# First FFN: smaller budgets for the side work per block and token tile, a booked adaLN extraction, and a defer shorter by one

## The chip, the cores and the metric

The kernel runs on one core of a Trainium2 chip. The metric is the device time of one execution in microseconds (us); three timed runs of the kernel before are shown below, and one execution was recorded by the hardware profiler. In the views PE is TensorE's matmul, DVE is VectorE, ACT is ScalarE, POOL is GpSimd and SP is SyncE, which issues most loads. DMAs are also issued from ScalarE's queue (ACTq in the rows).

## The reference, cut to what matters

One layer of a diffusion backbone over 1024 latent tokens and 256 context tokens, width 1024, in float32. The change lies in the first half-step SwiGLU (hidden width 2816) and in work that is done beside it:

```python
mx = adaln(c, w_mod[l], b_mod[l])            # nine rows of 1024: shift, scale, gate, three times
mc = adaln(c_ctx[None], w_mod[l], b_mod[l])
x = x + 0.5 * mx[2] * swiglu(modulate(x, g_ffn1[l], mx[0], mx[1]), w_gu1[l], w_down1[l])
ctx = ctx + 0.5 * mc[2] * swiglu(modulate(ctx, g_ffn1[l], mc[0], mc[1]), w_gu1[l], w_down1[l])
hx = modulate(x, g_mix[l], mx[3], mx[4])
...
x = x + mx[5] * mix_x                        # mixer: latent attention beside a bidirectional S5
x = x + 0.5 * mx[8] * swiglu(modulate(x, g_ffn2[l], mx[6], mx[7]), w_gu2[l], w_down2[l])
```

where `swiglu(h)` is `(silu(gate) * up) @ w_down` with `gate, up = split(h @ w_gu)`. The S5 branch needs tables of powers of its 16 x 64 complex states for both directions, made from parameters alone.

## The kernel before, in words

**The first FFN.** 1280 tokens are ten tiles of 128; three blocks `XB` hold four, four and two tiles. The hidden width is cut into `NF` = 22 blocks of 128, numbered f. For each f, gate and up (`gu`) are made transposed, 128 hidden rows by up to 512 tokens, over eight slices of the width. Each float32 product is three matmuls of high and low parts (`mm3`, L621 to L623 of the profile; wH, wL are a weight's parts, aH, aL those of an activation, hH, hL, shown as big, those of the input). ScalarE takes silu out of the gate's bank (sg), VectorE multiplies the up's bank into it (`sg<-gu,sg`), and ScalarE and GpSimd split the result. For every second f a `down` multiplies two hidden blocks by their down weights: ten tiles, two halves of 512 columns each, six matmuls for each half, and after each half VectorE adds the bank to the accumulator (`acc<-dn,acc`). In the loop, gate of f comes first, then the down of f-2 and f-1, if f is even, then the up of f. The last down, of f = 20 and 21 together (joint), comes behind the loop.

**The side work.** A generator `gen` in `ffn1_mix_in` holds the work that isn't the FFN's. First comes `adaln_rest`: seven rows of modulation (chunks 2 to 8), for which weight rows wmr are loaded and added, scaled, into ad on VectorE; TensorE sums over partitions (adp), and for the shift and scale rows `extract` multiplies by the identity and reduces (adm, then col). Then comes `s5_pre`: the power tables, and eight chunks of two S5 groups. A chunk makes a header (bc, B), a table T (six VectorE operations), for each direction d six products on GpSimd (tam, o1m, o2m) in turn with six on VectorE (taa, o1a, o2a), and a copy rep. `finish` of a direction then transposes and multiplies on TensorE (s5p, s5k), copies to me and R on ScalarE, and `store`, `diagonal` and `store_k` follow as deferred calls: three DMAs to d_s for a direction and four more for T, three small VectorE operations, and fifteen DMAs of R.

**What hands it out.** `pump(credit, cap)` adds to a credit, up to the cap, and runs the generator until the credit is spent; each `yield` names a price. It is called after each gu block with tiles * GURATE, and after each tile of a down with DNRATE. `defer(n, fn)` puts a call off by n calls of `side()`, one of which follows most pumps and each tile of a down. Before a chunk's header and before each direction's products the generator is held (`held`) until the finish before it has run. `drain()` runs all that is left at once. `at(20, 0)`, between the down of f = 20 and its up, drains, opens the pools of the gates g and of the residual rows xr in the memory that the side work's pools leave, and makes `prescale` the new generator: for each of ten tiles acc is multiplied by the gate and xr is added. `at(21, 1)` drains that, and the joint down follows.

Every instruction keeps its place in its engine's queue; nothing is reordered at run time.

Of the kernel before, what the change touches and what calls it, by code (L numbers as in the profile page):

```python
# [39 lines left out]
XLAG = 2  # L40
TLAG = 6
XB = [(0, 4), (4, 4), (8, 2)]
GURATE, DNRATE = 1.3, 1.2
SCRATCH = 512
PADR = 288

# [1 line left out]
class Kernel:  # L48
# [133 lines left out]
    def adaln_rest(self, pool):  # L182
        nc = self.nc
        wr, cols = {}, {}
        gates = (2, 5, 8)
        jobs = [(c, kt) for c in range(2, 9) for kt in range(KT + (c in gates))]

        def fetch(i):
            if i < len(jobs):
                c, kt = jobs[i]  # L190
                rows = (self.a["w_mod"][kt * 128:(kt + 1) * 128] if kt < KT else self.a["b_mod"])[:, c * D:(c + 1) * D]
                w = pool.tile([rows.shape[0], D], F32, tag="wmr", name="wmr", bufs=3)
                nc.sync.dma_start(w, rows)
                wr[i] = w

        def reduce(chunk, s, acc):
            row = chunk in gates
            m = pool.tile([1, D] if row else [128, D], F32, tag=f"adm{s}", name="adm")
            for h in range(2):
                p, hs = self.bank(self.free, "adp"), slice(h * 512, (h + 1) * 512)  # L200
                nc.tensor.matmul(p, lhsT=self.ones, rhs=acc[:, hs], start=True, stop=True)
                if row:
                    nc.scalar.activation(out=m[:, hs], in_=p[0:1, :], func=AF.Copy, scale=1.0 if chunk == 5 else 0.5)
                else:
                    nc.scalar.copy(m[:, hs], p)
            if row:
                self.defer(1, lambda: nc.scalar.dma_start(self.d_gate[chunk, s], m))
            else:
                self.defer(2, lambda: extract(chunk, s, m))

        def extract(chunk, s, m):
            c = self.cst.tile([128, KT], F32, name=f"col{chunk}{s}")
            v = m.rearrange("p (k f) -> p k f", k=KT)
            self.tt(v, v, self.ident[:, None, :].to_broadcast([128, KT, 128]), MUL)
            nc.vector.tensor_reduce(out=c, in_=v, axis=AX.X, op=ADD)
            self.tt(c, c, self.bcol[:, chunk, :], ADD)
            cols[chunk, s] = c
            if chunk in (4, 7):
                self.set_mod(1 if chunk == 4 else 2, s, cols[chunk - 1, s], c)

        fetch(0)
        fetch(1)
        accs = None
        for i, (chunk, kt) in enumerate(jobs):
            sets = (0, 1) if chunk <= 4 else (0,)
            if kt == 0:
                accs = [pool.tile([128, D], F32, tag=f"ad{s}", name=f"ad{s}") for s in sets]
            for s in sets:
                yield 1.2
                if s == 0:  # L230
                    fetch(i + 2)
                if kt == 0:
                    self.ts(accs[s], wr[i], self.sc[:, kt, s:s + 1], MUL)
                elif kt < KT:
                    self.stt(accs[s], wr[i], self.sc[:, kt, s:s + 1], accs[s], MUL, ADD)
                else:
                    self.tt(accs[s][0:1, :], accs[s][0:1, :], wr[i], ADD)
            wr.pop(i)
            if i + 1 == len(jobs) or jobs[i + 1][0] != chunk:
                for s in sets:  # L240
                    fn = lambda chunk=chunk, s=s, acc=accs[s]: reduce(chunk, s, acc)
                    self.defer(2 + s, fn)
                self.held = fn
                yield 2.5 * len(sets)
        while self.late:
            self.held = self.late[-1][1]
            yield 0.0


    def s5_pre(self, st):  # L250
# [185 lines left out]
        for c in range(G // GC):  # L436
# [35 lines left out]
            for d in range(2):  # L472
# [38 lines left out]
                def finish(d=d, dst=dst, M1=M1, M2=M2, AB=AB, AB2=AB2, rep=rep, T=T, Rs=Rs, c=c):  # L511
                    p = self.bank(self.free, "s5p")
                    for g in range(GC):
                        for i, X in enumerate((AB, AB2)):
                            nc.tensor.transpose(p[:, g * 256 + i * 128:g * 256 + i * 128 + 128],
                                                X[:, g].rearrange("p t c -> p (t c)"), self.ident)
                    me = pool.tile([128, GC, 256], F32, tag="me", name="me")
                    nc.scalar.copy(me.rearrange("p g n -> p (g n)"), p)
                    pk = self.bank(self.free, "s5k")
                    for g in range(GC):  # L520
                        nc.tensor.matmul(pk[:, g * 128:(g + 1) * 128], lhsT=rep[:, g].rearrange("p t c -> p (t c)"),
                                         rhs=M1[:, g, d:d + 8].rearrange("p t c -> p (t c)"), start=True, stop=True)
                    R = pool.tile([128, GC, 128], F32, tag=f"R{d}", name=f"R{d}")
                    nc.scalar.copy(R.rearrange("p g n -> p (g n)"), pk[:, 0:GC * 128])
                    Rs.append(R)
                    o = 1 - d

                    def store():
                        if d == 0:
                            for g in range(GC):  # L530
                                for h in range(2):
                                    nc.scalar.dma_start(
                                        dst[64 * h:64 * h + 64, g, O_T:O_T + 4 * NSEQ],
                                        T[64 * g:64 * g + 64].rearrange("p d r i j -> p (d r i j)"))
                        for i, X in enumerate((M1, M2)):
                            nc.scalar.dma_start(dst[:, :, O_C + d * 256 + i * 128:O_C + d * 256 + (i + 1) * 128],
                                                X[:, :, o:o + 8].rearrange("p g t c -> p g (t c)"))
                        nc.scalar.dma_start(dst[:, :, O_E + d * 256:O_E + d * 256 + 256], me)

                    def diagonal():  # L540
                        R0, R1 = Rs
                        self.tt(R0[:, :, 0:CH], R0[:, :, 0:CH], R1[:, :, 112:128], ADD)
                        for g in range(GC):
                            q = c * GC + g
                            self.stt(R0[:, g, 0:CH], mask, dsk[:, q:q + 1], R0[:, g, 0:CH], MUL, ADD)

                    def store_k():
                        R0, R1 = Rs
                        for s in range(8):
                            rows = slice(16 * s, 16 * s + 16)  # L550
                            nc.scalar.dma_start(dst[rows, :, O_K + 16 * s:O_K + 128], R0[rows, :, 0:128 - 16 * s])
                            if s:
                                nc.scalar.dma_start(dst[rows, :, O_K:O_K + 16 * s], R1[rows, :, 16 * (7 - s):112])

                    self.defer(1, store)
                    if d:
                        self.defer(2, diagonal)
                        self.defer(3, store_k)

                self.defer(4, finish)  # L560
                last = finish
        while self.late:
            self.held = self.late[-1][1]
# [89 lines left out]
    def ffn(self, blocks, hT, w_gu, w_dn, acc, P, hook=None, side=None, at=None, preload=None, keep=False, joint=False, start=None, pairs=0):  # L653
# [88 lines left out]
        for f in range(NF):  # L742
# [16 lines left out]
            else:  # L759
                sg = {}  # L760
                for b in nblk:
                    sg[b] = silu(b, gu(f, 0, b))
                    self.pump(blocks[b][1] * GURATE, 6.0)
                    if side:
                        side()
                load(f + 1, 0)
# [11 lines left out]
                    side()  # L778
                for b in nblk:
                    act[b] = act_of(f, b, sg[b], gu(f, 1, b))  # L780
                    self.pump(blocks[b][1] * GURATE, 6.0)
                    if side and f < NF - 2:
                        side()
                load(f + 1, 1)
# [10 lines left out]
    def ffn1_mix_in(self, srow):  # L795
# [24 lines left out]
        with ExitStack() as sact:  # L820
            actp = self.pool(sact, "act")
            with ExitStack() as sw:
# [75 lines left out]
                def at(f, phase):  # L898
                    if f == NF - 2 and phase == 0:
# [11 lines left out]
                        def prescale():  # L911
                            load(0)
                            load(1)
                            yield 4.0
                            for i, t in enumerate(order):
                                load(i + 2)
                                self.tt(acc[t], acc[t], g[int(t >= NX)], MUL)
                                yield 1.4
                                self.tt(acc[t], acc[t], xr.pop(i), ADD)
                                yield 1.4  # L920

                        self.gen = prescale()
                    elif f == NF - 1 and phase == 1:
# [901 lines left out]
```

## Time and profile before

| | us |
|---|---|
| three runs, median (lowest to highest) | 2546.02 (2544.89 to 2550.65) |
| profiled execution | 2544.01 |
| its span | 2542.2 |
| TensorE busy in the span | 2427.4 (95%) |
| VectorE busy | 1434.2 (56%) |
| granted TensorE clock, mean | 0.99 |

The profiled execution's time is that of the whole run; its span is the time from the first to the last recorded instruction, to which the times in the rows refer. TensorE's matmuls overlap: a row's duration runs from one matmul's start to its own modelled end, and the next starts before that.

### The profile page before, as it was taken

To read this page: it belongs to the slowest core of one execution; us is meant where nothing else is said; L and a number is where in the kernel's file an instruction comes from. 1 tells how busy PE (TensorE), PEld (TensorE's weight loads), DVE (VectorE), ACT (ScalarE), POOL (GpSimd) and SP (SyncE) were. 2 spreads that over 40 slices of the span, in tenths; PEclk is the share of its full clock that TensorE was granted. 3 is DMA by queue.
4 is the path that set the end of the run, shared out by engine and by line. 5 is a ranking of instruction groups with operands and counts; after the bars stand their busy time and mean duration, and the time that the engine had idled before them with its cause. 6 is when DMAs were issued, how large, how long until landed. Compare 5 with 4: busy or idle time off the path is not lost. (4 is left out here: it accounts for less than half of the span.)

```text
span 2542.2 us, 31980 instructions
## 1 busy us (share of the span) xinstructions
PE 2427.4 (95%) x12100; PEld 2004.9 (79%) x12100; DVE 1434.2 (56%) x2480; ACT 816.1 (32%) x1570; POOL 1036.1 (41%) x947
## 2 busy tenths in 40 slices
PE   7999998999999999898999999999999999999998
PEld 4788777888888887787777777777788888888886
DVE  3667578345434537747788888863344444444443
ACT  4311211211121112533677777762411111111112
POOL 2422314433433333426576666755433223323222
PEclk9999999999999999899999999999999999999999
DMA  7234621222222123316000000113211111111111
GB/s 283 86 106 135 205 83 38 71 70 59 75 71 71 57 79 126 123 38 192 23 17 4 14 14 25 38 66 126 75 44 49 50 50 50 50 45 46 50 42 67
DMA packets 83544, 185.14 MB, mean 73 GB/s; under 512 B 22199, under 2 KB 41911, under 8 KB 82366
## 3 DMA queue, kind: packets, MB, share of 16 engines
q1 hardware_dynamic: 59990, 163.93, 19.3%
q10 hardware_dynamic: 23400, 19.16, 2.6%
q8 instruction: 95, 1.56, 0.3%
q14 instruction: 59, 0.48, 0.1%
HBM read 155.52 MB, written 27.54 MB: 72 GB/s over the span
## 5 line engine op out<-in xcount | busy, mean ns | idle before, releaser
L62 POOL TENSOR_TENSOR wL<-raw,wH 128x1024 fp32r<-128x1024 f32 x130 | 313.8, 2418 | 787.6 <-ACT wH L616 776.5
L62 DVE TENSOR_TENSOR acc<-dn,acc 128x512 f32<-128x512 f32 x516 | 350.4, 690 | 352.3 <-PE dn L623 352.1
L621 PE MATMUL gu<-big,wH 128*128 128x512 f32 (+1 forms) x1056 | 379.9, 360 | 3.0 <-ACT sg L720 1.5
L623 PE MATMUL gu<-big,wL 128*128 128x512 f32 (+1 forms) x1056 | 374.8, 355 | 2.3 <-POOL wL L62 2.3
L622 PE MATMUL gu<-big,wH 128*128 128x512 f32 (+1 forms) x1056 | 374.6, 355 | 1.8 <-POOL big L62 1.8
L621 PE MATMUL dn<-wH,aH 128*128 128x512 f32 x792 | 314.6, 397 | 18.9 <-DVE acc L62 14.1
L623 PE MATMUL dn<-wH,aL 128*128 128x512 f32 x792 | 311.3, 393 | 1.0 <-POOL aL L62 1.0
L622 PE MATMUL dn<-wL,aH 128*128 128x512 f32 x792 | 311.4, 393 | 0.0
L616 ACT ACTIVATE wH<-raw 128x1024 fp32r<-128x1024 f32 x130 | 136.3, 1055 | 497.9 <-DVE raw L62 226.5
L62 DVE TENSOR_TENSOR sg<-gu,sg 128x512 f32<-128x512 f32 (+1 forms) x110 | 69.8, 635 | 391.7 <-PE gu L623 369.6
L622 PE MATMUL gu<-hL,wH 128*128 128x512 f32 x704 | 274.5, 390 | 4.3 <-POOL hL L62 3.0
L621 PE MATMUL gu<-hH,wH 128*128 128x512 f32 x704 | 274.6, 390 | 0.0
L623 PE MATMUL gu<-hH,wL 128*128 128x512 f32 x704 | 273.9, 389 | 0.0
L62 POOL TENSOR_TENSOR aL<-sg,aH 128x512 fp32r<-128x512 f32 (+1 forms) x110 | 140.4, 1277 | 277.5 <-ACT aH L616 275.0
L621 PEld LDWEIGHTS gu<-big,wH 128*128 128x128 f32 x1056 | 200.1, 189 | 36.0 <-issue 4.1
L623 PEld LDWEIGHTS gu<-big,wL 128*128 128x128 f32 x1056 | 199.9, 189 | 31.5 <-POOL wL L62 3.4
L622 PEld LDWEIGHTS gu<-big,wH 128*128 128x128 f32 x1056 | 200.1, 189 | 31.1 <-POOL big L62 2.2
L616 ACT ACTIVATE aH<-sg 128x512 fp32r<-128x512 f32 (+1 forms) x110 | 64.7, 589 | 461.6 <-DVE sg L62 425.0
L621 PEld LDWEIGHTS dn<-wH,aH 128*128 128x128 f32 x792 | 150.5, 190 | 54.4 <-DVE acc L62 15.8
L62 DVE TENSOR_TENSOR ptL<-pt,ptH 128x512 fp32r<-128x512 f32 x240 | 162.8, 686 | 52.2 <-ACT ptH L1417 51.7
L623 PEld LDWEIGHTS dn<-wH,aL 128*128 128x128 f32 x792 | 150.6, 190 | 33.6 <-POOL aL L62 1.4
L622 PEld LDWEIGHTS dn<-wL,aH 128*128 128x128 f32 x792 | 150.9, 191 | 31.1 <-issue 0.5
(317 smaller groups left out, 4635.7 us busy)
## 6 DMA issues: line engine op xcount, KB each, us to landing
raw<-in_w_gu SPq DMA_DIRECT2D x86, 512.0 KB, 3.4
wmr<-in_w_mod SPq DMA_DIRECT2D x56, 512.0 KB, 4.5
raw<-in_w_down SPq DMA_DIRECT2D x44, 512.0 KB, 3.3
row<-d_s SPq DMA_DIRECT2D x16, 576.0 KB, 4.0
wm<-in_w_mod SPq DMA_DIRECT2D x8, 1024.0 KB, 7.1
d_s<-T ACTq DMA_DIRECT2D x32, 160.0 KB, 2.7
ck<-d_s SPq DMA_DIRECT2D x16, 320.0 KB, 4.0
acc<-in_x SPq DMA_DIRECT2D x8, 512.0 KB
```

Of the source, the lines that this page charges most:

```text
L62: (eng or self.nc.vector).tensor_tensor(out=out, in0=a, in1=b, op=op)
L616: self.nc.scalar.activation(out=H, in_=raw, func=AF.Copy)
L621: mm(out, lhsT=AH, rhs=BH, start=start, stop=False)
L622: mm(out, lhsT=AH, rhs=BL, start=False, stop=False)
L623: mm(out, lhsT=AL, rhs=BH, start=False, stop=stop)
```

## The change

Two rates are lowered (per tile of a gu block 1.3 to 1.1, per tile of a down 1.2 to 0.9), and the cap of a gu block goes from 6.0 to 4.0. `extract` now books 2.7 from the credit and `diagonal` 0.6, where they booked nothing; a scaled add of adaLN is priced 1.5 instead of 1.2. `finish` is put off by three calls of `side()` instead of four. The prices in `prescale` fall from 4.0, 1.4 and 1.4 to 3.0, 1.0 and 1.0. No operation is added or removed; the side work's instructions stand elsewhere among those of the FFN. The second FFN has no generator. The whole diff:

```diff
--- before.py
+++ after.py
@@ -40,7 +40,7 @@
 XLAG = 2
 TLAG = 6
 XB = [(0, 4), (4, 4), (8, 2)]
-GURATE, DNRATE = 1.3, 1.2
+GURATE, DNRATE = 1.1, 0.9
 SCRATCH = 512
 PADR = 288
 
@@ -211,6 +211,7 @@
         def extract(chunk, s, m):
             c = self.cst.tile([128, KT], F32, name=f"col{chunk}{s}")
             v = m.rearrange("p (k f) -> p k f", k=KT)
+            self.credit -= 2.7
             self.tt(v, v, self.ident[:, None, :].to_broadcast([128, KT, 128]), MUL)
             nc.vector.tensor_reduce(out=c, in_=v, axis=AX.X, op=ADD)
             self.tt(c, c, self.bcol[:, chunk, :], ADD)
@@ -226,7 +227,7 @@
             if kt == 0:
                 accs = [pool.tile([128, D], F32, tag=f"ad{s}", name=f"ad{s}") for s in sets]
             for s in sets:
-                yield 1.2
+                yield 1.5
                 if s == 0:
                     fetch(i + 2)
                 if kt == 0:
@@ -539,6 +540,7 @@
 
                     def diagonal():
                         R0, R1 = Rs
+                        self.credit -= 0.6
                         self.tt(R0[:, :, 0:CH], R0[:, :, 0:CH], R1[:, :, 112:128], ADD)
                         for g in range(GC):
                             q = c * GC + g
@@ -557,7 +559,7 @@
                         self.defer(2, diagonal)
                         self.defer(3, store_k)
 
-                self.defer(4, finish)
+                self.defer(3, finish)
                 last = finish
         while self.late:
             self.held = self.late[-1][1]
@@ -760,7 +762,7 @@
                 sg = {}
                 for b in nblk:
                     sg[b] = silu(b, gu(f, 0, b))
-                    self.pump(blocks[b][1] * GURATE, 6.0)
+                    self.pump(blocks[b][1] * GURATE, 4.0)
                     if side:
                         side()
                 load(f + 1, 0)
@@ -778,7 +780,7 @@
                     side()
                 for b in nblk:
                     act[b] = act_of(f, b, sg[b], gu(f, 1, b))
-                    self.pump(blocks[b][1] * GURATE, 6.0)
+                    self.pump(blocks[b][1] * GURATE, 4.0)
                     if side and f < NF - 2:
                         side()
                 load(f + 1, 1)
@@ -911,13 +913,13 @@
                         def prescale():
                             load(0)
                             load(1)
-                            yield 4.0
+                            yield 3.0
                             for i, t in enumerate(order):
                                 load(i + 2)
                                 self.tt(acc[t], acc[t], g[int(t >= NX)], MUL)
-                                yield 1.4
+                                yield 1.0
                                 self.tt(acc[t], acc[t], xr.pop(i), ADD)
-                                yield 1.4
+                                yield 1.0
 
                         self.gen = prescale()
                     elif f == NF - 1 and phase == 1:
```

The first place is VectorE's queue in the down of f = 6, where the tiles' evictions `acc<-dn,acc` and the adaLN sums of a chunk alternate. Before:

```order
L62 TENSOR_TENSOR acc<-dn,acc 128x512 x2
L69 SCALAR_TENSOR_TENSOR ad_2390<-wmr,sc,ad_2390 128x1024
L62 TENSOR_TENSOR adm<-adm,ident 128x1024
L215 TENSOR_REDUCE col_2462<-adm 128x8
L62 TENSOR_TENSOR col_2462<-col_2462,bcol 128x8
L69 SCALAR_TENSOR_TENSOR ma_2466<-col_2462,gcol 128x8
L62 TENSOR_TENSOR acc<-dn,acc 128x512 x2
```

In the changed kernel, the same down:

```order
L62 TENSOR_TENSOR acc<-dn,acc 128x512 x4
L69 SCALAR_TENSOR_TENSOR ad_2370<-wmr,sc,ad_2370 128x1024
L62 TENSOR_TENSOR acc<-dn,acc 128x512 x2
L69 SCALAR_TENSOR_TENSOR ad_2370<-wmr,sc,ad_2370 128x1024
L62 TENSOR_TENSOR acc<-dn,acc 128x512 x4
L69 SCALAR_TENSOR_TENSOR ad_2370<-wmr,sc,ad_2370 128x1024
```

The product with the identity, the reduce and the two short column operations behind it have left this place; scaled adds stand alone between evictions.

The second place is the end of the down of f = 20 on TensorE, where its last matmuls meet the up (gu) of f = 20, and where `at(20, 0)` drains. Before:

```order
L621 MATMUL dn<-wH_7237,aH_7366 128x512
L622 MATMUL dn<-wL_7238,aH_7366 128x512
L623 MATMUL dn<-wH_7237,aL_7367 128x512
L621 MATMUL gu<-big,wH_7372 128x512
L622 MATMUL gu<-big,wH_7372 128x512
L623 MATMUL gu<-big,wL_7373 128x512
```

In the changed kernel, whose line numbers here are higher by two:

```order
L624 MATMUL dn<-wL_7052,aH_7186 128x512
L625 MATMUL dn<-wH_7051,aL_7187 128x512
L516 MATMUL s5p<-ident,o1a 128x128
L516 MATMUL s5p<-ident,o2a 128x128
L516 MATMUL s5p<-ident,o1a 128x128
L516 MATMUL s5p<-ident,o2a 128x128
L522 MATMUL s5k<-o1m,rep 128x128 x2
L516 MATMUL s5p<-ident,o1a 128x128
L516 MATMUL s5p<-ident,o2a 128x128
L516 MATMUL s5p<-ident,o1a 128x128
L516 MATMUL s5p<-ident,o2a 128x128
L522 MATMUL s5k<-o1m,rep 128x128 x2
```

Three finishes (four transposes and the kernel products each, of directions 1, 0 and 1) now stand between dn and gu.

The third place is ScalarE's queue there. Before, it has the last stores of R of chunk 7 (d_s_7), and then the splits of f = 20 and 21 and the silu of f = 21 (L720):

```order
L551 DMA d_s_7_114<-R_7251 32x1x16
L553 DMA d_s_7_114<-R_7467 32x1x112
L616 ACTIVATE wH_7670<-raw 128x1024
L616 ACTIVATE aH_7700<-sg 128x512
L616 ACTIVATE aH_7737<-sg 128x512
L616 ACTIVATE aH_7775<-sg 128x256
L616 ACTIVATE wH_7785<-raw 128x1024
L720 ACTIVATE sg<-gu 128x512 x2
L720 ACTIVATE sg<-gu 128x256
```

In the changed kernel the rows are these; they begin with the last two stores of R of chunk 6 (d_s_6), and the fifteen stores of R of chunk 7 follow them, ahead of wH and aH:

```order
L553 DMA d_s_6_113<-R_7337 32x1x16
L555 DMA d_s_6_113<-R_7523 32x1x112
L519 COPY me<-s5p 128x512
L525 COPY R_7594<-s5k 128x256
L533 DMA d_s_7_114<-T 64x640 x4
L537 DMA d_s_7_114<-o1m 256x1x128
L537 DMA d_s_7_114<-o2m 256x1x128
L539 DMA d_s_7_114<-me 256x1x256
L519 COPY me<-s5p 128x512
L525 COPY R_7633<-s5k 128x256
L537 DMA d_s_7_114<-o1m 256x1x128
L537 DMA d_s_7_114<-o2m 256x1x128
```

What stood at this place, the splits of f = 20, now stands behind both chunks' stores.

## Rows read from the trace of the kernel before

**Rows 1.** The page's first line.

```profile
span 2542.2 us, 31980 instructions
```

**Rows 2.** Windows: stretch, length, busy PE, PEld, DVE, ACT, POOL, clock, DMA share, GB/s.

```profile
105.00:450.00 345.00, 327.16 (x1533) 267.78 (x1532) 250.12 (x470) 55.80 (x85) 98.34 (x83) 0.98 0.35 114
450.00:956.60 506.60, 506.60 (x2569) 432.53 (x2569) 218.94 (x394) 85.36 (x140) 198.58 (x163) 1.00 0.24 72
956.60:1001.00 44.40, 42.80 (x222) 36.09 (x220) 33.25 (x27) 7.45 (x13) 15.81 (x9) 1.00 0.36 117
```

**Rows 3.** PE's waits, 100 to 450: total us, times, longest.

```profile
PE dn L621 <- DVE acc L62: 14.1, 4, 7.6
```

**Rows 4.** PE's timeline: start, us, engine, line, operation, count, [idle before <-releaser].

```profile
135.88 0.40 PE L621 MATMUL dn<-wH,aH 128*128 128x512 f32 x1
...
176.86 1.88 PE L201 MATMUL adp<-ad,ones 128*128 128x512 f32 x4
178.18 0.79 PE L621 MATMUL gu<-big,wH 128*128 128x512 f32 x1
...
424.06 0.79 PE L621 MATMUL dn<-wH,aH 128*128 128x512 f32 x1 [7.59 <-DVE acc L62]
...
472.68 0.27 PE L515 MATMUL s5p<-ident,o1a 128*128 128x128 f32 x1
...
473.48 0.36 PE L621 MATMUL gu<-big,wH 128*128 128x256 f32 x1
...
504.87 0.40 PE L621 MATMUL dn<-wH,aH 128*128 128x512 f32 x1
...
589.02 0.40 PE L621 MATMUL dn<-wH,aH 128*128 128x512 f32 x1
```

**Rows 5.** DVE's timeline: reduce, evictions at the table steps, products without and beside POOL.

```profile
238.52 1.22 DVE L215 TENSOR_REDUCE col<-adm 128x8 f32<-128x1024 f32 x1
...
423.33 1.26 DVE L62 TENSOR_TENSOR acc<-dn,acc 128x512 f32<-128x512 f32 x2
...
441.18 0.43 DVE L62 TENSOR_TENSOR o1a<-pwB,B 128x256 f32<-128x256 f32 x1
...
912.77 0.93 DVE L62 TENSOR_TENSOR taa<-pwB,B 128x256 f32<-128x256 f32 x1
```

**Rows 6.** PE's and DVE's timelines between the down of f=20 and the joint down.

```profile
956.17 0.39 PE L623 MATMUL dn<-wH,aL 128*128 128x512 f32 x1
...
968.16 1.22 DVE L62 TENSOR_TENSOR acc<-acc,xr 128x1024 f32<-128x1024 f32 x1
...
994.32 3.30 DVE L62 TENSOR_TENSOR acc<-acc,xr 128x1024 f32<-128x1024 f32 x1
...
1000.98 0.50 PE L623 MATMUL dn<-wH,aL 128*128 128x512 f32 x1 [1.00 <-POOL aL L62]
```

**Rows 7.** ACT's timeline in chunk 7; the last row: L551's issues, shortest/median/longest in ns.

```profile
928.92 0.58 ACT L518 COPY me<-s5p 128x512 f32<-128x512 f32 x1
...
938.80 1.25 ACTq L551 DMA_DIRECT2D d_s<-R  x2
...
947.81 1.30 ACTq L553 DMA_DIRECT2D d_s<-R  x1
...
L551 ACTq DMA_DIRECT2D d_s<-R x64: 555/602/642, 513.3 to 947.2; - x64
```

**Rows 8.** SP's waits and timeline, 900 to 1010; DMA issues (count, size, us to landing).

```profile
SPq L792 <- DMA d_s<-R: 24.4, 2, 24.2
...
949.61 2.19 SPq L909 DMA_DIRECT2D xr<-in_ctx  x2
...
d_s<-me ACTq DMA_DIRECT2D x16, 256.0 KB, 2.5
...
xr<-in_ctx SPq DMA_DIRECT2D x2, 512.0 KB, 5.5
...
d_s<-R ACTq DMA_DIRECT2D x8, 16.0 KB, 1.9
```

## The prediction

> **What bounds the kernel now.** I read the page's head and the windows first, then the waits and the timelines of the places where they show a loss. The span is 2542.2 us [rows 1]; the profiled execution took 2544.01 us, 1.8 more than its span, and 2.0 less than the median of 2546.02. All sums below are made against 2544.0, and 2 us are added at the end. 0.2% of this time, 5.1 us, is about what a measurement here can tell from no change.
>
> The windows [rows 2] cut the first FFN into three parts. From 105 to 450 TensorE is busy 327.16 of 345 us: 17.8 are idle. From 450 to 956.6 it is busy all 506.6, so nothing there can be won. From 956.6 to 1001, the up of f=20 and both halves of f=21, 42.8 of 44.4. So only the first window, where the adaLN rows and the tables are the side work, has something to give. The waits say which: 14.1 of the idle time is dn waiting for VectorE's acc eviction, four times, the longest 7.6 [rows 3].
>
> The loss is larger than the waits. Downs stand every second f; from the down of f=2 (135.88) to that of f=10 (504.87) are four intervals, 368.99 us together, and the next one, without a stall, is 84.15 [rows 4]. Four clean ones are 336.6, so the excess is 32.4. Part of it is honest work: eight adaLN sums on TensorE (each 1.32, from 176.86 to 178.18), 10.6 us. But the clean interval has two chunk finishes in it (472.68 to 473.48, 0.80, with the weight load 0.87 each), and the four have two, where four clean ones would have eight: six fewer, 5.2. Stalls and what follows them (the matmul at 424.06 takes 0.79, others 0.40) are 32.4 - 10.6 + 5.2 = 27.0 us. That is the most the change can win.
>
> **What the change wins: G.** The causes are readable. In the down of f=6 the extraction stands among the evictions: a product and a reduce of 1.22 each (238.52, [rows 5]) with nothing booked for them. The clean interval, less two finishes, is 82.4 us for 360 matmuls of 512 columns (240 of gu, 120 of dn; the short block counted as half ones), 0.229 each, so a tile of twelve takes TensorE 2.7. VectorE spends 1.26 on the tile's two evictions [rows 5], and a budget of 1.2 gives it one scaled add per tile, a pass over 128x1024 like the reduce, 1.22: 2.5 of 2.7. An extraction on top of that puts it behind. At f=8 the table steps stand before the eviction of 423.33, and dn waits 7.59 [rows 4, 5]. In the changed order the row of f=6 is one add between evictions, with extraction and reduce gone from the down. Credit per pair of f falls from 2(26)+12 = 64 to 2(22)+9 = 53, and 2.7 are booked per extraction, so a tile gets a step at most, and not each tile one. I take G = 25, with 27 as the upper end and 20 as the lower: at f=8 and f=10 the down may still meet one late weight row or one table step held by GpSimd, and the 3.7 of the 17.8 idle that are not waits for acc need not be cured. The adaLN step's 1.5 and the shorter defer of 3 cost no instruction; they only move the steps.
>
> **What the change loses: C.** With 53 instead of 64 credits per pair the generator is no longer done when `at(20, 0)` calls `drain()`. Before, the last evictions and the gu of f=20 stand next to each other. In the changed order there are three finishes between them on TensorE, and on ScalarE the storing of chunks 6 and 7, 43 DMA issues, ahead of wH and all aH of f=20. The side work is the same; it now stands where nothing covers it, since prescale can only start behind it: g and xr take the SBUF of the chunk pools, and SyncE already waits there, 24.2 us for d_s<-R [rows 8].
>
> I count from T0, the end of the last dn of f=20 (956.17 + 0.39 = 956.56, [rows 6]). Last eviction 0.7 and nine header operations on 64 columns, estimated at 0.17 from a quarter of the 256-column product (0.43, [rows 5]) and a fixed part: 2.2. Then six table and six cross products on VectorE; alone 0.43 to 0.5 each, beside GpSimd's products 0.93 (912.77, [rows 5]). At 0.93 they end at 13.4, at 0.45 at 7.6. The rep copy and the three operations of the diagonal of chunk 6, 0.9 estimated: 14.3, or 8.5. ScalarE's store_k of chunk 6, fifteen issues, takes what that of chunk 7 takes now, 938.80 to 947.81 + 1.30: 10.3 [rows 7], so 24.6. The next R copy must wait for the landing (1.9, [rows 8]) and takes 0.4, estimated from the me copy of twice its size, 0.58: 26.9. The store of chunk 7, direction 0, is four T issues and three others, seven at 0.602 [rows 7], 4.2: 31.1. The me copy waits for that me's landing, 2.5 from its issue (1.9 after the issue's end): 33.0, and the me and R copies make it 34.0. Store of direction 1, three issues, 1.8: 35.8 is where store_k of chunk 7 starts. From there to the first xr issue are 10.8 now (938.80 to 949.61): 46.6. Landing 5.5 [rows 8]: 52.1. From the first xr add at 968.16 to the start of the joint down, which last waits for aL at 1000.98, are 32.8 now [rows 6]: 84.9. Now it is 1000.98 - 956.56 = 44.4. The shift is 40.5; three finishes at 0.87 were on TensorE before as well and leave the path elsewhere, so 37.9 is the upper end.
>
> The lower end: 0.45 instead of 0.93 (5.8 less), and prescale without GpSimd's two holds (an add of 3.30 where the others take 1.22, [rows 6]; two of them 4.2) since TensorE and GpSimd are idle by then: 27.9. I take C = 35: the 0.93 is the row of the same operation beside the same GpSimd products, so I keep it, and about half of the holds go, since the splits of f=21 will be done earlier.
>
> A rule stands against so long a chain. The Trainium skill, DMA: Bandwidth & Descriptors, section Anatomy of one DMA, puts the sequencer's dispatch of a DMA at some 50 ns and most of the fixed 2 us in the write's receipt (it says this of the GpSimd path). By it 43 issues would take 2 us, and C would be about 12. In this trace one issue on ScalarE takes 0.555 at the least and 0.602 in the median over 64 [rows 7], so the sum goes by the row.
>
> **Net:** 2544.0 - 25 + 35 = 2554, and with the 2 us to the median 2556.
>
> **Rivals.** *Drain as forecast, at its cheap end*: C = 28 with G = 25 to 27 gives +1 to +3, 2547 to 2549, no difference. For it: 0.93 holds only while GpSimd works, some 11 us of the stretch. Against it: the DMA issues are most of the chain and their price is well known. 0.17. *Faster: prescale has slack.* If the first xr lands by T0 + 42 instead of 52 (say the gate and xr loads wait for fewer stores than I read), C falls below 25 and the sign turns. What stays at the least is TensorE's own wait for the last cross product: eighteen table and cross operations, of which those behind GpSimd's twelve products (0.88 each, 2.2 + 10.6 = 12.8) run at 0.45, end at 16, so gu is taken up at 17.8, 15 late without the finishes; -25 + 15 = -10: 2536. For it: TensorE is idle only 1.6 of 44.4 there now [rows 2]. Against it: SyncE's 24.2 for d_s<-R, and that the joint down's first matmuls wait for aL already [rows 6, 8]. 0.12. *Cheap issues*: if ScalarE's 43 issues could go out in a few us, as the lower bound of 12 has it, the net is -13, 2533. The row of 0.602 speaks against it; 0.03. *No relief:* the stalls of 105 to 450 only move to other tiles, since what isn't in the downs is in the gu blocks, where VectorE's sg products free the gu banks. G = 10, net +25: 2571. For it: a gu block of 512 tokens gives 4 credits at once, 4 us of VectorE work before an sg. Against it: the waits of that window hold no gu that waits for VectorE, at a cap of 6. 0.08. *Drain and relief as forecast*, 0.60, its own range 2551 to 2564 (G 20 to 27, C 30 to 38).
>
> **Chances.** Slower by over 0.2%: 0.60 + 0.08 = 0.68. Within: 0.17. Faster: 0.15. The range reaches from the cheap drain, with room for part of the case between it and slack (2543), to the case of no relief (2571); the 0.15 of faster and a little at the top are left out.
>
> **What would show it.** In the changed trace: dn waits for acc between 105 and 450 fall from 14.1 to under 3, and the down of f=10 starts near 479 instead of 504.87. The joint down starts about 82 after the last dn of f=20, with TensorE idle some 35 of these; the first xr is issued 46 after it, not 7 before it; the granted clock falls there. Behind it, nothing changes. It would be wrong if the start of the joint down follows the drain by under 70, or if the first window keeps its stalls.

## The result, and the profile after

The changed kernel takes 2565.02 us (median of four, 2563.51 to 2565.61), against 2547.3 for the kernel before, run beside it: a ratio of 1.0068, 95% interval 1.005 to 1.0085, 17.7 us slower. Forecast were 2556 and slower. The profiled execution took 2565.24, its span 2563.4, 21.2 more than that of [rows 1]; the profiled execution of the kernel before lay 3.3 below its median, so the spans differ by more than the medians.

The windows of the changed kernel, cut as in [rows 2] (the columns are the same):

```profile
105.00:450.00 345.00, 345.00 (x1660) 286.04 (x1659) 213.36 (x263) 60.67 (x92) 91.91 (x48) 1.00 0.36 117
450.00:956.60 506.60, 490.35 (x2458) 416.40 (x2458) 275.34 (x601) 80.27 (x130) 202.35 (x197) 0.98 0.20 60
956.60:1001.00 44.40, 29.48 (x141) 25.02 (x140) 17.84 (x16) 4.33 (x8) 7.98 (x4) 0.85 0.53 166
```

TensorE is now busy all 345 us of the first window, where 17.8 were idle; in the second, where nothing was idle, 16.3 are, and in the third 14.9 of 44.4. So the idle time of the first window is gone, all of it, and something larger has opened behind it. Four rows of TensorE's timeline place it: the start of the down of f=10, the end of the down of f=20, the start of the up of f=20 behind the drained finishes, and the sixth matmul of the joint down. The sixth is the matmul that [rows 6] show at 1000.98 and to which the prediction counts; "the start of the joint down" means it from here on:

```profile
480.03 0.40 PE L623 MATMUL dn<-wH,aH 128*128 128x512 f32 x1
...
937.04 0.39 PE L625 MATMUL dn<-wH,aL 128*128 128x512 f32 x1
...
954.93 0.77 PE L623 MATMUL gu<-big,wH 128*128 128x512 f32 x1
...
1022.48 0.50 PE L625 MATMUL dn<-wH,aL 128*128 128x512 f32 x1
```

Against [rows 4, 6] the change divides into three parts:

| part | before | after | difference | without the finishes that moved (0.87 each) |
|---|---|---|---|---|
| to the down of f=10 | 504.87 | 480.03 | -24.8 | -23.1 (two fewer) |
| from there to T0, the end of the last dn of f=20 | 451.7 | 457.4 | +5.7 | +6.6 (one fewer) |
| T0 to the start of the joint down | 44.4 | 85.0 | +40.6 | +38.0 (three more) |
| sum | | | +21.5 | +21.5 |

The spans differ by 21.2: from the joint down on the changed kernel takes as long as the kernel before, to 0.3. The longest waits of TensorE from 470 to 960 and then from T0 to the joint down (total, times, longest) say what the last two parts are:

```profile
PE s5p L516 <- DVE o1a L62: 11.0, 3, 9.0
PE s5p L516 <- DVE o2a L62: 3.5, 3, 2.1
PE dn L623 <- DVE acc L62: 1.7, 2, 1.3
```

```profile
PE gu L623 <- ACT wH L618: 12.8, 1, 12.8
PE s5p L516 <- DVE o1a L62: 9.5, 2, 9.0
PE gu L623 <- DVE sg L62: 3.4, 1, 3.4
PE s5p L516 <- DVE o2a L62: 2.7, 2, 2.1
```

The 9.0 is the first drained finish of chunk 7, waiting for the cross products that `drain()` handed out at once. The 12.8 is the up of f=21, waiting for the split of its weights. ScalarE's queue shows the chain between them; a row of a DMA issue is the time of issuing alone:

```profile
951.24 1.26 ACTq L553 DMA_DIRECT2D d_s<-R  x2
...
961.10 0.60 ACTq L555 DMA_DIRECT2D d_s<-R  x1
961.74 0.59 ACT L519 COPY me<-s5p 128x512 f32<-128x512 f32 x1 [22.97 <-DMA d_s<-R]
962.41 0.37 ACT L525 COPY R<-s5k 128x256 f32<-128x256 f32 x1
962.43 2.44 ACTq L533 DMA_DIRECT2D d_s<-T  x4
...
968.88 0.59 ACT L519 COPY me<-s5p 128x512 f32<-128x512 f32 x1 [6.10 <-DMA d_s<-me]
...
970.95 1.25 ACTq L553 DMA_DIRECT2D d_s<-R  x2
...
1001.21 1.06 ACT L618 ACTIVATE wH<-raw 128x1024 fp32r<-128x1024 f32 x1 [5.92 <-DMA raw<-in_w_gu]
```

Fifteen stores of chunk 6 from 951.24 to 961.70, the copy of the finish that TensorE had done long before, seven stores, a copy that waits for the landing, three stores, and fifteen of chunk 7 from 970.95. SyncE's queue carries on from there:

```profile
977.38 0.96 SPq L794 DMA_DIRECT2D g<-d_gate  x2
...
981.83 1.66 SPq L911 DMA_DIRECT2D xr<-in_ctx  x2
984.19 12.13 SPq L911 DMA_DIRECT2D xr<-in_x  x4
996.38 0.42 SPq L665 DMA_DIRECT2D raw<-in_w_gu  x1
```

The weights of f=21 (raw, 996.38) stand behind four xr loads, of which the last three each wait until an addition of prescale has freed a buffer (issued at 988.98, 993.40 and 996.00, when additions end at 988.96, 993.37 and 995.97); hence the 12.8. VectorE's prescale itself runs from 982.99 to 1015.84.

### The profile page after: what moved, and what is told of

It reads as the page before. It is cut to its first block, busy times and chain, and to the rows that moved or that the text cites. A ratio compares the mean times of both kernels' runs of the same rounds, so it can differ in the third digit from the quotient of the medians.

```text
span 2563.4 us, 31993 instructions
## 1 busy us (share of the span) xinstructions
PE 2434.2 (95%) x12100; PEld 2011.7 (78%) x12100; DVE 1449.8 (57%) x2480; ACT 818.2 (32%) x1570; POOL 1034.8 (40%) x947
## 5 line engine op out<-in xcount | busy, mean ns | idle before, releaser
L623 PE MATMUL gu<-big,wH 128*128 128x512 f32 (+1 forms) x1056 | 383.6, 363 | 18.8 <-ACT wH L618 12.8
L623 PEld LDWEIGHTS gu<-big,wH 128*128 128x128 f32 x1056 | 203.0, 192 | 51.9 <-ACT wH L618 13.0
L624 PEld LDWEIGHTS gu<-big,wH 128*128 128x128 f32 x1056 | 203.3, 193 | 30.6 <-POOL big L62 1.6
L624 PEld LDWEIGHTS dn<-wL,aH 128*128 128x128 f32 x792 | 149.7, 189 | 31.1 <-issue 1.0
```

The costliest lines, as they stand in the source:

```text
L623: mm(out, lhsT=AH, rhs=BH, start=start, stop=False)
L624: mm(out, lhsT=AH, rhs=BL, start=False, stop=False)
```

## The experiments

The theory after this reading: the gain is in the downs up to f=8, and the loss is the drain, by a chain of DMA issues on ScalarE. The rival: the thinner budgets and the other edits cost time in themselves, and the drain has slack.

**The drain alone.** The kernel before, with the side work stopped for three f, so that the drain holds what it holds in the changed kernel:

```diff
 def down(fs, tiles, post):
+    rate = 0.0 if fs[-1][0] + 1 in (17, 18, 19) else DNRATE
...
-        self.pump(DNRATE, DNRATE)
+        self.pump(rate, rate)
...
-self.pump(blocks[b][1] * GURATE, 6.0)
+self.pump(blocks[b][1] * (0.0 if f in (17, 18, 19) else GURATE), 6.0)
```

> The kernel before with the side work paused from f=17 to f=19, so that the drain at f=20 holds what it holds in the changed kernel: three finishes, 43 DMA issues on ScalarE, and nothing else is moved before f=17. Theory (the drain is the loss): the joint down starts 84 us after the last dn of f=20 instead of 44, and the time is 2547 + 37 = 2584, between 2579 and 2588. Rival (the drain has slack, and the changed kernel loses its time to the thinner budgets elsewhere): within 5 of 2547.

Measured: 2589.8 us, ratio 1.0169 (1.0154 to 1.0184), 43 slower, and 2 above the upper end expected. The last dn of f=20 and the last wait of the joint down's start, on TensorE:

```profile
954.75 0.39 PE L623 MATMUL dn<-wH,aL 128*128 128x512 f32 x1
...
1042.42 0.50 PE L623 MATMUL dn<-wH,aL 128*128 128x512 f32 x1 [1.00 <-POOL aL L62]
```

From T0 = 955.14 to the joint down are 87.3, 42.9 more than before; without the three finishes, 40.3. The rival is out. The 40.3 are 2 more than the changed kernel's 38.0. The two differ there in the budgets behind f=20 and in the prices of prescale, which come below; what makes the 2 was not tried. What the traces show is that prescale's twenty operations on VectorE, 1.22 each alone, are held by 9.8 in all in this kernel, by 6.3 in the changed one and by 5.9 in the kernel before.

**One part of the change each.** The bookings alone (2.7 in `extract`, 0.6 in `diagonal`); the rates alone (1.1 and 0.9); and the rest alone (1.5 for an add, defer of 3, prescale 3.0, 1.0, 1.0). The cap of 4.0 is in none of the three.

> The kernel before with nothing but the bookings of 2.7 for an extraction and 0.6 for a diagonal. The drain then holds 6.6 credits: the second half of the last chunk, one finish and some 25 DMA issues less than in the changed kernel. Theory: a smaller drain costs less, store_k of chunk 7 can start some 10 us after the last dn instead of 33.5, so the drain costs about 15; if the booking is what cures the downs, the down of f=10 starts at 485 or before and the time is 2540 to 2550; if the lower rates cure them, it starts near 500 and the time is 2556 to 2564.

> The kernel before with nothing but the rates 1.1 and 0.9 (cap 6.0, no booking). The drain holds 9.2 credits and two finishes: store_k of chunk 7 can start some 14 us after the last dn, the drain costs 18 to 20. If the rates cure the downs, the down of f=10 starts at 485 or before and the time is 2545 to 2552; if it is the booking, it starts near 500 and the time is 2560 to 2567.

> The kernel before with the rest of the change alone: the adaLN add priced 1.5, finish put off by three calls instead of four, the prices of prescale 3.0, 1.0 and 1.0. The side work is done at f=18 already. Theory (these parts move steps and cost nothing): within 4 of 2547. Rival (a shorter defer packs the chunks closer, and ScalarE's stores and GpSimd's products come in the way of wH and wL, as in the run with late rates): 2553 or more, with waits of gu for wH or wL.

Measured: 2547.64, ratio 1.0001 (0.9992 to 1.001); 2562.23, ratio 1.0063 (1.0048 to 1.0078); 2541.13, ratio 0.9981 (0.9972 to 0.999). The first row below is the start of the down of f=10 with the bookings alone, the second with the rates alone; the third is from the kernel with other prices of prescale (below), whose code is that of the kernel before up to f=20:

```profile
487.37 0.40 PE L623 MATMUL dn<-wH,aH 128*128 128x512 f32 x1
```

```profile
502.43 0.40 PE L621 MATMUL dn<-wH,aH 128*128 128x512 f32 x1
```

```profile
512.70 0.40 PE L621 MATMUL dn<-wH,aH 128*128 128x512 f32 x1
```

The bookings alone bring 17.5 of the 24.8, the rates alone 2.4. The start of f=10 scatters, though: three executions of the same code up to there (before, the paused kernel and the one of the third row) have it at 504.87, 506.15 and 512.70, five of the changed kernel's code at 478.64 to 480.03. The 17.5 is clear of that, the 2.4 is not: of the parts tried alone only the bookings bring much. (The rates' drain of 9.2 credits costs 22.4 to the joint down, 66.8 against 44.4, expected 18 to 20.) With the booking the last dn of f=20 ends at 938.68, as early as in the changed kernel; the smaller drain (6.6 credits) costs 19.7 us to the joint down (64.1 against 44.4), where I had expected 15, and the two cancel. The third kernel was 6 us faster, which neither side had, and its trace does not explain it: the profiled execution lay 3.7 above the median, and in it the down of f=10 starts 4.0 earlier and the last dn of f=20 ends 3.0 earlier, neither clear of the scatter. The joint down then starts 48.4 behind that, 3.9 more than before, which the next run takes up. What made the 6 stays open.

**The prices of prescale.**

> The kernel before with nothing but the prices of prescale, 3.0, 1.0 and 1.0. In three runs with an empty drain and these prices the joint down started 47.5 after the last dn of f=20 and gu waited for wH and wL of f=21. Theory (these prices bring that wait, as more of prescale is issued ahead of the loads of f=21): the joint down starts 47.5 after the last dn, and the time is 2549 to 2552. Rival (it comes from the other parts): 44.4, and within 2 of 2547.

Measured: 2549.63, ratio 1.0011 (1.0002 to 1.002). The profiled execution lay 6.6 above its median, so only distances in it are used: the joint down starts 48.4 after the last dn (964.39 to 1012.77), 4.0 more than before. (The 47.5 of the expectation goes to the fourth matmul of the joint down, here 47.56, where the kernel before has 42.7; so the 44.4 of the rival is of another matmul than the 47.5. The theory holds either way.) SyncE's queue, in this kernel and then in the kernel before, says why:

```profile
959.91 26.68 SPq L909 DMA_DIRECT2D xr<-in_x  x6
986.64 0.43 SPq L663 DMA_DIRECT2D raw<-in_w_gu  x1
```

```profile
953.27 22.56 SPq L909 DMA_DIRECT2D xr<-in_x  x4
975.91 0.38 SPq L663 DMA_DIRECT2D raw<-in_w_gu  x1
```

With lower prices two more xr loads are issued ahead of the weights of f=21, and these go out 22.2 instead of 19.4 after the last dn. Here gu waits for them, 0.7 for wH and 2.4 for wL. Whether the same prices help behind a long drain, where the joint down started 2 earlier with them than without, was not tried by itself.

**The gain without the drain.** The changed kernel with higher rates from f=11 on:

```diff
 def down(fs, tiles, post):
+    rate = 1.2 if fs[-1][0] + 1 >= 11 else DNRATE
...
-        self.pump(DNRATE, DNRATE)
+        self.pump(rate, rate)
...
-self.pump(blocks[b][1] * GURATE, 4.0)
+self.pump(blocks[b][1] * (1.6 if f >= 11 else GURATE), 7.0 if f >= 11 else 4.0)
```

> The changed kernel, but from f=11 on the rates are 1.6 per tile of a gu block, with a cap of 7.0, and 1.2 per tile of a down; the side work is then done at f=19 and the drain is empty. Theory (the gain is in the downs up to f=10, the loss is the drain): the first windows keep their gain and the drain's 37 us are gone: 2524 to 2531, and the joint down starts 44 us after the last dn of f=20. Rival (a higher rate in the gu blocks brings its own waits, of gu for sg): 2537 or more, with waits of gu for VectorE from 560 on.

Measured: 2541.65, ratio 0.998 (0.997 to 0.999): 5 us gained, where 16 to 23 were expected. What took the rest is a mechanism that neither side had named. The waits of TensorE from 560 to 950, and ScalarE's queue ahead of the first of them:

```profile
PE gu L625 <- POOL wL L62: 3.4, 2, 1.7
PE gu L623 <- ACT wH L618: 2.3, 2, 1.2
```

```profile
787.56 1.24 ACTq L553 DMA_DIRECT2D d_s<-R  x2
...
796.57 0.60 ACTq L555 DMA_DIRECT2D d_s<-R  x1
797.22 1.06 ACT L618 ACTIVATE wH<-raw 128x1024 fp32r<-128x1024 f32 x1 [9.25 <-PE gu L625]
```

Where a chunk's `store_k` falls between the gate and the up of an f, its fifteen issues stand 9.6 us ahead of the split that the next gu needs. Each of the two intervals in which that happens is 92.1 from down to down, against 85.1 to 85.7 for its neighbours. Of the 6 to 7 more, 2.9 are these waits; behind them the matmuls are slow (granted clock 0.72 from 795 to 806, 1.00 from 740 to 795). And the joint down starts 50.2 after the last dn of f=20 instead of 44.4, with waits of 3.3 for wH and 1.3 for wL of f=21.

**Which early budget.** The changed kernel with the gu blocks' 1.3 and 6.0 restored and 0.9 for downs only up to f=8 (1.2 from f=10 on); and the same with 0.3 for the down of f=8, 1.2 from f=9 on and a cap of 4.0 for the blocks of f=7 to 9.

> The changed kernel with the gu blocks' rate and cap as before (1.3, 6.0), 0.9 per tile of a down only up to f=8, and 1.2 from f=10 on. The side work is done at f=19, the drain is empty, and from f=10 on no budget is above that of the kernel before. Theory (the gain is in the downs up to f=8, the loss is the drain, and the higher gu budget brought the waits for wH and wL in the run with late rates): the down of f=10 starts at 486 or before, the joint down 44 after the last dn of f=20, 2524 to 2532. Rival (whatever is gained before f=10 is lost again behind it, because the same side work stands in fewer f): 2538 to 2546, with waits of gu for wH and wL between f=12 and f=20.

> As the run with the changed rate of the downs alone, but the down of f=8, where the tables start, gets 0.3 per tile, and the gu blocks of f=7 to 9 a cap of 4.0, so that few table steps stand among evictions. Theory (a table step ahead of evictions is what is left of the waits): no dn wait for acc above 0.5 before f=10, 2 to 4 us less than that run, 2521 to 2529. Rival: the tables' steps wait in the gu blocks or behind them just as long, and the time is the same as that run's within 2.

Measured: 2549.23, ratio 1.0007 (0.9998 to 1.0016), and 2552.96, ratio 1.0027 (1.0017 to 1.0036). Both theories of mine failed. In the first the down of f=10 starts at 496.35. The first row is the worst wait of that kernel, in the down of f=8, which starts at 405.47; then come the two costliest groups on VectorE from 389 to 416, ahead of that down's first evictions (count, busy us, mean ns), and the longest operation among them:

```profile
416.91 0.79 PE L623 MATMUL dn<-wH,aH 128*128 128x512 f32 x1 [5.81 <-DVE acc L62]
```

```profile
L66 DVE TENSOR_SCALAR q<-q 128x64 f32<-128x64 f32 (+1 forms) x40 | 9.4, 243 | 1.2
L62 DVE TENSOR_TENSOR q<-q,q 128x64 f32<-128x64 f32 (+1 forms) x33 | 9.0, 275 | 0.8
```

```profile
407.44 2.28 DVE L66 TENSOR_SCALAR q<-q 128x64 f32<-128x64 f32 x1
```

The table steps that the gu blocks hand out, small operations on 32 and 64 columns, fill VectorE from 389.7 to 416.2 (busy 24.1 of 26.5 us) and are still running when the down begins. Three of them are held long, to 1.24, 2.33 and 2.28 where their like take 0.2, each beside a subtraction on GpSimd (the last beside the split of a weight, 407.20 to 409.66): some 5 of the 26 us. In the second kernel the wait at f=8 is 0.31, but one of 10.63 stands at f=10, where the last table steps and the first chunk's products are ahead of the evictions, and the sum of an adaLN chunk waits 8.97 for its last addition at 381.82: the steps were only put off. A down's own rate isn't the lever there; the blocks' budget is: up to f=10 the changed kernel differs from the first of the two in the blocks' rate and cap alone, and its down of f=10 starts 16.3 earlier. It has 1.26 left of this wait, at f=10, behind a step held to 2.42. With finishes left out, the booking alone gives 16.6 of the 23.1 to the down of f=10 (17.5, less one finish that moved); the first kernel here, which has the bookings too, gives 6.8, so the parts do not add up. How much each of rate, cap, price and defer gives of the 6.5 that the booking alone leaves stays open.

**The chain of issues.** The changed kernel with the seven stores of R1 of chunks 6 and 7 issued from SyncE:

```diff
-nc.scalar.dma_start(dst[rows, :, O_K:O_K + 16 * s], R1[rows, :, 16 * (7 - s):112])
+(nc.sync if c > 5 else nc.scalar).dma_start(dst[rows, :, O_K:O_K + 16 * s], R1[rows, :, 16 * (7 - s):112])
```

> The changed kernel, in which the seven stores of R1 of chunks 6 and 7 are issued from SyncE instead of ScalarE. Theory (the drain is a chain of DMA issues, 0.64 each, on ScalarE): store_k of chunk 6 takes some 5.3 instead of 10.5, store_k of chunk 7 starts 5 earlier and lets the first xr go 4 earlier still, so the joint down starts 9 to 10 earlier: 2554 to 2558. Rival (what lasts is the landing, or SyncE's own order): within 3 of 2565.

Measured: 2557.94, ratio 1.0044 (1.003 to 1.0058), 7 less than the changed kernel. ScalarE's start of the stores of chunk 7 and SyncE's first xr:

```profile
963.83 5.83 ACTq L553 DMA_DIRECT2D d_s<-R  x8
```

```profile
969.83 1.20 SPq L911 DMA_DIRECT2D xr<-in_ctx  x2
```

T0 is 934.67: the stores of chunk 7 start at 29.2 (33.5 in the changed kernel), the first xr at 35.2 (44.4). The chain is 9.2 shorter, as expected; the joint down starts at 78.3, only 6.7 earlier where 9 to 10 were expected, since prescale and f=21 behind it take 2.5 longer.

**A version that keeps the gain.** First the bookings alone with dense downs from f=12 on; then the changed kernel up to f=10, with dense downs and a lower cap than before from f=11 on, and the old prices of prescale; then the same with all stores of R1 on SyncE. The second one's edit:

```diff
 def down(fs, tiles, post):
+    rate = 1.6 if fs[-1][0] + 1 >= 11 else DNRATE
...
-        self.pump(DNRATE, DNRATE)
+        self.pump(rate, rate)
...
-self.pump(blocks[b][1] * GURATE, 4.0)
+self.pump(blocks[b][1] * (1.3 if f >= 11 else GURATE), 5.0 if f >= 11 else 4.0)
...
-yield 3.0
+yield 4.0
...
-yield 1.0
+yield 1.4
```

> The kernel before with the two bookings, and from f=12 on with 1.6 per tile of a down and a cap of 5.0 for a gu block, so that the drain is empty. Theory (booking cures the extraction's waits, the drain costs what stands in it, and in the chunks VectorE has room in the downs while a gu block's budget must not rise): the down of f=10 starts at 487, no gu waits for wH or wL, the last dn of f=20 ends near 940 and the joint down starts 44 later: 2527 to 2535. Rival (the same side work in fewer f brings waits wherever it stands): 2539 to 2546.

> The changed kernel up to f=10; from f=11 on 1.3 per tile of a gu block with a cap of 5.0, and 1.6 per tile of a down, and the prices of prescale as before (4.0, 1.4, 1.4). The drain is empty. Theory: the gain up to f=10 stays (f=10's down at 480), the waits of wH and wL that the run with late rates had do not come, since the gu blocks' budget is not above that before, and the joint down starts 44.4 after the last dn: 2522 to 2531. Rival (dense chunks bring these waits in any case): 2538 to 2545.

> The run before (slow up to f=10, then dense downs), with the seven stores of R1 of every chunk issued from SyncE instead of ScalarE. In that run the only wait of gu between f=12 and f=20 was for wH and wL at 796, where fifteen stores of R, 9.9 us, stood right ahead of wH on ScalarE. Theory (these issues hold wH): with eight instead of fifteen that wait is gone, and with it some 6 us of the interval in which it stands (90.3 between the downs of f=16 and f=18): 2522 to 2526. Rival (SyncE's loads of weights now stand behind the stores, and come late instead): 2530 or more, with waits of gu for wH whose releaser is a load.

Measured: 2537.36, ratio 0.9958 (0.9946 to 0.9971); 2529.87, ratio 0.9933 (0.992 to 0.9947); 2525.09, ratio 0.9913 (0.9896 to 0.9929). The first has the waits for wH and wL in two intervals (at 717 and 890), so it lies between its two expectations. The windows of the second, cut at the last dn of f=20 and the start of the joint down:

```profile
105.00:450.00 345.00, 345.00 (x1661) 286.17 (x1660) 214.88 (x270) 60.82 (x92) 93.24 (x48) 1.00 0.35 115
450.00:941.10 491.10, 485.08 (x2445) 412.39 (x2444) 281.55 (x597) 81.42 (x133) 203.66 (x197) 1.00 0.23 67
941.10:986.40 45.30, 43.10 (x222) 36.16 (x220) 33.42 (x27) 8.11 (x13) 18.31 (x9) 1.00 0.50 169
```

The drain is gone (45.3 where the changed kernel has 85.0) and the first window's gain is kept. TensorE's waits of this kernel from 546 to 940 are those for the weights again, once:

```profile
PE gu L625 <- POOL wL L62: 1.7, 1, 1.7
PE gu L623 <- ACT wH L618: 0.7, 1, 0.7
```

In the third kernel neither is left from 540 to 940, and the interval from f=16 to f=18 is 85.95 instead of 90.3. That settles it: the issues ahead of wH held it. No gu waits for a late load of weights there either, as its rival had it.

## Why the prediction was right, and where it was off

**Direction and loss: right in mechanism, and near in size.** C was forecast at 35, with 28 and 37.9 as its ends; it measured 38.0. The chain came in the order counted, each step but the last 0.3 to 3.5 early (us after T0; T0 is 937.43):

| step | counted at its upper end | measured |
|---|---|---|
| six table and six cross products done | 13.4 | 12.5 |
| diagonal of chunk 6 done | 14.3 | 13.8 |
| store_k of chunk 6 issued | 24.6 | 24.3 |
| next R copy done | 26.9 | 25.4 |
| store of chunk 7, direction 0, issued | 31.1 | 29.5 |
| me and R copies done | 34.0 | 32.3 |
| store_k of chunk 7 starts | 35.8 | 33.5 |
| first xr issued | 46.6 | 44.4 |
| first xr add starts | 52.1 | 48.6 |
| joint down starts | 84.9 | 85.0 |

That the last row agrees to 0.1 is luck: the first xr add was 3.5 early, and the stretch from there to the joint down, counted at the 32.8 of the old trace, became 36.4. The value of 35 was 3 low. I took half of GpSimd's holds off that stretch (2.1 of 37.9, which leaves 35.8, not 35), but the holds did not go: they are 6.3 in all against 5.9 before. And the end of that stretch is not set by prescale alone, as I had it: prescale was done at 1015.84, and TensorE's up of f=21 only at 1020.6, since its weights stood behind xr loads on SyncE. The old trace had that order in SyncE's queue too, but there it cost nothing.

**The Trainium skill's rule on a DMA's dispatch.** Fifteen issues took 10.46 us in the changed kernel, 0.70 each, and moving seven of each fifteen of chunks 6 and 7 to another queue took 9.2 off the chain. The 50 ns that the Trainium skill, DMA: Bandwidth & Descriptors, section Anatomy of one DMA, gives for the sequencer's dispatch is said of GpSimd's path, which no run here used; for ScalarE's queue the measurement decides, and the rival of cheap issues, 2533, is out.

**The gain: mis-sized.** G was 25, with 20 as its lower end; it measured 16.5 (23.1 - 6.6), so this term is what put the sum out most: 8.5 of the 11 us between the forecast +10 and the 21.2 of the spans, C the other 3. To the down of f=10 it is 23.1, within my range. What I left out is what the stages that move later bring with them: I read the second window as one in which nothing could be won, and did not ask what could be lost there. The table steps, delayed by the lower budget, now meet the down of f=10 (1.26), and the first chunk's finish waits for its products at 543 (1.53 and 0.80); with 0.47 at 663 that is 4.1 of waits. The matmuls behind them run slow (granted clock 0.91 from 540 to 560), which I estimate at the rest of the 6.6.

**What cures the downs: half right.** The step named the unbooked extraction and a lower budget per tile. The extraction was right (17.5 by booking alone). The tile's rate was not: 0.9 in the downs with the old gu budget, the bookings, the 1.5 and the defer of 3 starts f=10 at 496.35, later than the booking alone. The gu blocks' budget, which the step has only in its credit per pair (and there without the cap of 4.0, which can cut the 4.4 of a block of four tiles), is worth 16.3. What the down finds on VectorE is what the gu blocks ahead of it left there.

**"The adaLN step's 1.5 and the shorter defer of 3 cost no instruction; they only move the steps":** true of the count (VectorE has 2480 instructions before and after); the 3.0 by which the last dn of f=20 ended earlier with the rest alone is not clear of the scatter. The prices of prescale, which the sum didn't name, cost 4.0 to the joint down with an empty drain.

**The rivals.** Slack in the drain: out, the first xr was issued only at 44.4 and would have had to land by 42. TensorE did take up gu 17.5 after T0, as that rival had it (17.8), but this was not what ended last. No relief: out, the first window has no idle time. The measured 2565 lies 1 above the range of the case that came true (2551 to 2564), and inside the whole range by the part that was kept for no relief, a case that did not come: the direction was argued, the hit on the range was in part luck.

**The signs.** No dn waits for acc from 105 to 450, where under 3 us were forecast; f=10's down starts at 480.03 (479); the joint down starts 85.0 after T0 (82), with TensorE idle for 30.1 of these (35) at a granted clock of 0.78, where it had 1.00; behind it, nothing changes.

## What to carry to other kernels

A budget that hands out side work has two ends: lowering it to protect the evictions is paid where a `drain()` collects what is left, and there each DMA issue, landing and buffer release of a chain that was hidden is on the path. So count the credits to the end of the generator before changing a rate, and try the booking of what isn't booked by itself: here it brought most of the gain, but it fills the drain too (6.6 credits, 19.7 us, which ate it up). And look at what stands ahead of a weight's split or load in its queue: fifteen small stores ahead of a split, and two more loads ahead of a load, each cost some 4 us.

## What the runs showed of the hardware

Two things that I had not expected at this size. A split behind a block of DMA issues in ScalarE's queue started only when the last of them was out: with late rates wH starts at 797.22, right behind the fifteenth store (796.57 and 0.60), and with eight of fifteen stores left on its queue, the wait for wH at 796 was gone. An operation ahead of an issue goes on beside it, as the R copy of 962.41 and the T stores from 962.43 show. And the doubling of VectorE's products beside GpSimd's, which the prediction took from one row, held for the whole stretch: eleven products on 320 and 256 columns took 0.80 to 1.01 each from 939.97 on in the changed kernel, and six of the same on 256 columns took 0.42 each from 951.12 on, with GpSimd idle. One of each, of the same shape:

```profile
947.20 1.01 DVE L62 TENSOR_TENSOR o2a<-pwB,B 128x256 f32<-128x256 f32 x1
...
952.25 0.42 DVE L62 TENSOR_TENSOR o2a<-pwB,B 128x256 f32<-128x256 f32 x1
```
